# A tenth unit in the first phase, a third group buffer for one raw tile, later dt and gate transposes, first sums on VectorE

## The chip, the cores and the metric

The kernel runs on one core of a Trainium2 chip. The metric is the device time of one execution in microseconds (us). All tensors are float32 in HBM. Every weight is split on the core into a high and a low part, and each product is made of three matmuls.

## The reference, cut to what matters

Two layers work on 256 tokens of width 2048. Each layer scales and shifts its normalised input by values that come from a conditioning vector `c` through a large matrix `ada_w` (2048 by 6144), then runs a token mixer and a projection back.

```python
cond = silu(c)
for i in range(2):
    shift, scale, gate = split(cond @ ada_w[i] + ada_b[i], 3)
    h = rmsnorm(x, norm_w[i]) * (1 + scale) + shift
    out = ssd_mixer(h) if i == 0 else mlstm_mixer(h)
    x = x + gate * out
return rmsnorm(x, final_norm_w)

# ssd_mixer: proj = h @ w_in gives z, x, B, C (causal conv and silu on x, B, C) and dt
dt = softplus(dt + dt_bias); a = -exp(a_log) * dt      # per head; cumulated over tokens
y  = chunked scan over (x*dt, a, B, C) + d_skip * x    # 8 groups of 8 heads
out = rmsnorm_per_group(y * silu(z)) * norm_w @ w_out

# mlstm_mixer: proj = h @ w_in gives q, k, v, o, z and two gate rows per head
log_f = log_sigmoid(f_pre + b); decays from cumulated log_f and i_pre
out = (per-head norm of sigmoid(o) * chunked attention) * silu(z) @ w_out
```

## The kernel before

The weights arrive as loads of 512 KB, `raw` tiles of 128 by 1024 floats, on the queue of SyncE (SP). `RAWB` says how many raw tiles there are. A weight tile is split by ScalarE (`hi`, line 78, in `act`) and VectorE (`lo`, line 86, in `vtt`); there are four buffers of each. TensorE then runs 24 matmul triples of 256 columns for one half of an item (lines 304 to 306). An `ada` tile isn't split: VectorE multiplies it by a column of `cond` and adds it to the accumulator `aacc` (line 82, in `stt`).

Everything is one list of items, in `items`. A unit is four blocks of 128 output columns over the whole depth of 2048; it has four items of 1 MB (two loads each). In layer 0 the units are `z`, `x` (per group of eight heads) and `bc` (B and C of two groups).

- The first phase runs through the depth in four stages (`START`). A stage needs four chunks of the normalised input, `hT`, and these need eight `ada` items to be added up, transposed and summed (`total`, lines 233 to 257). Within a stage each unit of the list `PRE` gets one item, and the `ada` items of the next stage lie between them. The first two units of `PRE` stay in PSUM; of the others, each stage's part is added by VectorE to a `park` tile in SBUF. Those parked tiles are taken from the four `y` buffers, two units to a tile.
- The dt unit runs at the front of the last stage. `dt_done` makes softplus, decay and cumulated sums on VectorE, then transposes them on TensorE (lines 570 to 572).
- `POST` lists what follows: the other units and the output passes (`op`), with `ada` items (third entry of a token) spread among them. The scan of a group needs its `xs` tile, tag `s4b`, handed out in order of groups.
- Layer 1 begins in the same way, with the list `K1` and 16 late `ada` items among its items; `gates_done` is its counterpart to `dt_done`, with transposes on line 872.

Steps that belong to no matmul are generators. `run_bg` takes one step of each before every half item, so `yield from lag(n)` puts the next step n halves later in the program. The order on each engine is made from the program by a scheduler that can move a step ahead again; `tc.high_priority` puts what is written under it first. The engines then run their instructions in order.

Of the kernel before, what the change touches and what calls it, by code (L numbers as in the profile page):

```python
# [13 lines left out]
P = 128  # L14
T = 256
# [10 lines left out]
for _n, _w in _VEC:  # L26
# [6 lines left out]
START = [4, 4, 4, 4]  # L33
K1 = [("o", 0), ("z", 0), ("qk", 0), ("v", 0), ("qk", 1), ("v", 1), ("o", 1), ("z", 1)]
RES1, DEF1, GPOS = 2, 16, 0
PRE = [('x', 0), ('bc', 0), ('z', 0), ('x', 1), ('bc', 1), ('bc', 2), ('z', 1), ('x', 2), ('z', 2)]
RES = 2
RAWB, HIB, E6B = 6, 4, 2
HP_SPLIT = (False, None)
HP_OP = (True, None)  # L40
CONV_STT, NW_STT, Y_STT, OP_STT, X_DVE = True, False, False, True, False
ROWLAG = 4
LOOK_LOAD, LOOK_SPLIT, HALF_US, BG_LIM, BG_MIN, DEBT_CAP = 3, 3, 2.56, 3.0, 5, 2.0
HP_H = (True, None)
POST = [('z', 4), ('z', 3, (0, 1)), ('x', 3, (0, 1)), ('x', 4, (0, 2)), ('z', 5, (0, 2)), ('x', 5, (0, 2)),
        ('op', (0, 1, 2), (0, 8)), ('bc', 3), ('x', 6, (1, 1)), ('z', 6, (1, 1)), ('x', 7, (1, 1)), ('z', 7, (1, 1)),
        ('op', (3, 4), (1, 4)), ('op', (5, 6, 7), (1, 8))]

# [2 lines left out]
def trunk_kernel(ctx, tc, xt, vecs, ada, wdt, wss, wso, wgt, wml, wmo, fnw, result):  # L51
# [12 lines left out]
    def nm(s):  # L64
        uid[0] += 1
        return f"{s}{uid[0]}"
# [131 lines left out]
            gens.insert(0, b)  # L198
        return b

    slots = {"s4a": 2, "s4b": 2, "s4c": 2}

    def take(tag):
        yield from gate_ok(lambda: slots[tag] > 0)
# [9 lines left out]
    def ada_work(it):  # L214
        layer, key, q, w = it["layer"], it["key"], it["q"], it["w"]
        per = 1024 // w
        if q == 0:
            finish(sums)
            acc_tiles[layer, key] = sp.tile([P, 1024], F32, tag="adaacc", name=nm("aacc"), bufs=1)
        acc = acc_tiles[layer, key][:, 0:w]  # L220
        for k in range(2 * per * q, 2 * per * (q + 1)):
            raw = it["raw"][(k // per) % 2][:, (k % per) * w:(k % per + 1) * w]
            if k == 0:
                vts(acc, raw, cond[:, 0:1], None, ALU.mult)
            else:
                stt(acc, raw, cond[:, k:k + 1], acc, ALU.mult, ALU.add)
        if q != it["nq"] - 1:
            return
        if key < 4:
            spans = [(4 * key, 4), (16 + 4 * key, 4)]  # L230
        else:
            spans = [(32 + 8 * (key - 4), 4), (36 + 8 * (key - 4), 4)]
        def total():
            yield
            sm = sp.tile([P, 8], F32, tag="asum", name=nm("asum"))
            ps = [misc() for _ in spans]
            c = 0
            for t, (o, n) in zip(ps, spans):
                for b in range(n):
                    nc.tensor.transpose(t[:, b * P:(b + 1) * P], acc[:, (c + b) * P:(c + b + 1) * P], ident)  # L240
                c += n
            c = 0
            for t, (o, n) in zip(ps, spans):
                both = layer == 0 and key < 4 and c == 0
                if both:
                    nc.vector.tensor_reduce(sm[:, 0:n], t.rearrange("p (b t) -> p b t", b=4), axis=mybir.AxisListType.X,
                                            op=ALU.add)
                for b in range(0 if both else n):
                    sl = slice(b * P, (b + 1) * P)
                    act(t[:, sl], t[:, sl], AF.Copy, accum_out=sm[:, c + b:c + b + 1])  # L250
                m = mod[layer][:, o:o + n]
                vtt(m, sm[:, c:c + n], vec(f"ab{layer}", o, n), ALU.add)
                c += n
                known.update((layer, o + b) for b in range(n))
                if 16 <= o < 32:
                    stt(amul[layer][:, o - 16:o - 16 + n], m, 1.0, vec(f"nw{layer}", o - 16, n), ALU.add, ALU.mult)
            yield
        sums.append(spawn(total()))
# [288 lines left out]
    def dt_done(banks):  # L547
        def g():
            bk = banks[0][:, 0:T]
            rw = sp.tile([P, 4, T], F32, tag="a4", name="dtrow")  # L550
            dt, tmp = rw[:, 0, :], rw[:, 1, :]
            vts(tmp, bk, vec("dtb"), None, ALU.add)
            softplus(tmp, dt)
            yield
            na = sp.tile([P, 1], F32, tag="na", name="na", bufs=1)
            act(na, vec("alog"), AF.Exp)
            vts(na, na, -1.0, None, ALU.mult)
            vts(tmp, dt, na, None, ALU.mult)
            for c in range(2):
                s = slice(c * P, (c + 1) * P)  # L560
                nc.vector.tensor_tensor_scan(acs[:, s], ones, tmp[:, s], 0.0, ALU.mult, ALU.add)
            nc.gpsimd.dma_start(acd, acs[0:64, :])
            slots.update(a4=1, e6=2)
            spawn(gen_rows())
            cr = tmp[:, 0:P]
            vts(cr, acs[:, 0:P], -1.0, acs[:, P - 1:P], ALU.mult, ALU.add)
            yield
            p1, p2 = misc(), misc()
            for c in range(2):
                nc.tensor.transpose(p1[:, c * P:(c + 1) * P], dt[:, c * P:(c + 1) * P], ident)  # L570
                nc.tensor.transpose(p2[:, c * P:(c + 1) * P], acs[:, c * P:(c + 1) * P], ident)
            nc.tensor.transpose(p2[:, 2 * P:3 * P], cr, ident)
            give("a4")
            vts(dtT, p1[:, 0:T].rearrange("p (c h) -> p c h", c=2)[:, :, 0:64],
                                    0.5, None, ALU.mult)
            nc.vector.tensor_copy(acT, p2[:, 0:384].rearrange("p (c h) -> p c h", c=3)[:, :, 0:64])
            spawn(gen_decay())
            yield
        held["dt"] = spawn(g())
# [23 lines left out]
    def xs_done(g):  # L603
        def f(banks):
            def conv():
                yield from gate_ok(lambda: g == 0 or g - 1 in taken)
                yield from take("s4b")
                taken.add(g)
                xs_t[g] = sp.tile([P, 4, T], F32, tag="s4b", name=nm("xs"))
                yield from gen_conv(banks, "scw", "scb", [4 * g + b for b in range(4)], xs_t[g])  # L610
            x_done[g] = hold(spawn(conv()), banks)
            held[0, g] = spawn(gen_ssd(g))
        return f
# [233 lines left out]
    def gates_done(banks):  # L847
        def g():
            bk = banks[0][:, 0:T]
            rw = sp.tile([P, 4, T], F32, tag="a4", name="gaterow")  # L850
            xx, lf = rw[:, 0, :], rw[:, 1, :]
            ip = sp.tile([P, T], F32, tag="t1", name="ip", bufs=3)
            vts(xx, bk, vec("gb"), None, ALU.add)
            nc.vector.memset(ip, 0.0)
            act(ip[0:8, :], xx[32:40, :], AF.Copy)
            yield
            vts(xx, xx, -1.0, None, ALU.mult)
            softplus(xx, lf)
            yield
            vts(lf, lf, -1.0, None, ALU.mult)  # L860
            for_scan = sp.tile([P, T], F32, tag="t1", name="onesr", bufs=3)
            nc.vector.memset(for_scan, 1.0)
            bc = xx
            nc.vector.tensor_tensor_scan(bc, for_scan, lf, 0.0, ALU.mult, ALU.add)
            vtt(ip, ip, bc, ALU.subtract)
            nc.vector.tensor_tensor_scan(G, ip, ip, 0.0, ALU.max, ALU.max)
            nc.gpsimd.dma_start(Gd, G[0:8, :])
            vtt(lf, bc, G, ALU.add)
            yield from lag(6)
            p1, p2 = misc(), misc()  # L870
            for c in range(2):
                nc.tensor.transpose(p1[:, c * P:(c + 1) * P], lf[:, c * P:(c + 1) * P], ident)
                nc.tensor.transpose(p2[:, c * P:(c + 1) * P], ip[:, c * P:(c + 1) * P], ident)
            act(eT, p1[:, 0:T].rearrange("p (c h) -> p c h", c=2)[:, :, 0:8], AF.Exp, scale=-1.0)
            vts(ncT, p2[:, 0:T].rearrange("p (c h) -> p c h", c=2)[:, :, 0:8], -1.0, None, ALU.mult)
            yield
        held["gates"] = spawn(g())
# [27 lines left out]
    def o_done(h):  # L905
        def f(banks):
            head_over(h)
            to_t[h] = sp.tile([P, 4, T], F32, tag="s4b", name=nm("to"))
            for i in range(2):
                act(to_t[h][:, 2 * i:2 * i + 2, :], pair(banks[i]), AF.Tanh, scale=0.5)  # L910
        return f
# [94 lines left out]
    for q in range(4):  # L1006
# [4 lines left out]
        for j, w in enumerate(new):  # L1011
            if q == 3 and j == GPOS:
                add_unit(Unit("fm", 1, 8, 1, h_act, gates_done), [wgt])
            items.append(w)
            n = -(-len(late) // max(1, len(new) - j + (2 - q) * len(new))) if q < 3 and (q, j) >= (0, 3) else 0
            items.extend(late[:n])
            late = late[n:]
    assert not late
# [24 lines left out]
    def prep(j):  # L1043
        n, half = halves[j]
        it = items[n]
        if it["kind"] == "h":
            finish(sums)
            for k in it["ks"]:
                h_chunk(it["layer"], k)
            return  # L1050
        while nload[0] < min(len(loads), it["ln"] + LOOK_LOAD):
            load(loads[nload[0]])
# [114 lines left out]
```

## Time and profile before

| what | value |
|---|---|
| three runs | 1775.24 us median, 1775.02 to 1779.06 |
| profiled execution, its time | 1770.52 us |
| its span, first to last instruction | 1768.7 us |
| TensorE (PE) busy | 1679.2 us, 95% |
| VectorE (DVE) busy | 1301.9 us, 74% |
| ScalarE (ACT) busy | 923.3 us, 52% |
| read from HBM | 400.89 MB |
| mean granted clock of TensorE | 0.98 of full speed |

The profiled execution was 4.7 us faster than the median of the runs. TensorE is nearly always busy, so the time can only fall where TensorE waits, and it waits in the first half of the span for the most part. The two numbers to hold side by side in a stretch are the busy times of TensorE and VectorE.

### The profile page before, as it was taken

To read this page: it belongs to the slowest core of one execution; us is meant where nothing else is said; L and a number is where in the kernel's file an instruction comes from. 1 tells how busy PE (TensorE), PEld (TensorE's weight loads), DVE (VectorE), ACT (ScalarE), POOL (GpSimd) and SP (SyncE) were. 2 spreads that over 40 slices of the span, in tenths; PEclk is the share of its full clock that TensorE was granted. 3 is DMA by queue.
4 is the path that set the end of the run, shared out by engine and by line. 5 is a ranking of instruction groups with operands and counts; after the bars stand their busy time and mean duration, and the time that the engine had idled before them with its cause. 6 is when DMAs were issued, how large, how long until landed. Compare 5 with 4: busy or idle time off the path is not lost.

```text
span 1768.7 us, 32784 instructions
## 1 busy us (share of the span) xinstructions
PE 1679.2 (95%) x13285; PEld 1623.4 (92%) x13285; DVE 1301.9 (74%) x1639; ACT 923.3 (52%) x1551; POOL 35.6 (2%) x55
## 2 busy tenths in 40 slices
PE   2998979999999999989998999999999999999997
PEld 2998969998999999989888989899999898989997
DVE  7889978998986888867977986766556565564554
ACT  3443558788874674444445554544344444454433
POOL 0000000000000000000000000000000000000000
PEclk6999989999999999999999999999999999999998
DMA  9989745686876667958974567777555555565551
GB/s 358 338 311 320 275 161 179 213 280 226 280 284 207 220 219 254 337 167 307 328 249 153 203 229 246 254 246 246 182 181 178 181 175 184 188 196 169 189 180 71
DMA packets 111048, 405.20 MB, mean 229 GB/s; under 512 B 12440, under 2 KB 12448, under 8 KB 110896
## 3 DMA queue, kind: packets, MB, share of 16 engines
q1 hardware_dynamic: 107568, 391.50, 64.6%
q0 software_dynamic: 3040, 10.56, 2.0%
q8 instruction: 104, 1.70, 0.4%
q10 hardware_dynamic: 288, 1.05, 0.1%
q14 instruction: 48, 0.39, 0.1%
HBM read 400.89 MB, written 2.17 MB: 228 GB/s over the span
## 4 chain that ended last, share of the span: by engine, by line
PE 73%; issue 9%; DVE 8%; DMA 7%; ACT 2%; POOL 0%; SPq 0%; POOLq 0%; DVEq 0%; ACTq 0%
PE pj L304 18%; PE pj L305 18%; PE pj L306 18%; DMA raw<-in_ada 4%; DVE aacc L82 3%; DVE lo L86 3%; PE ms L304 2%; PE ms L305 2%; PE ms L306 2%; PE pj L315 2%; PE pj L317 2%; PE pj L316 2%; DMA raw<-in_wml 1%; ACT hi L78 1%; PE ms L697 1%
## 5 line engine op out<-in xcount | busy, mean ns | idle before, releaser
L78 ACT ACTIVATE hi<-raw 128x1024 fp32r<-128x1024 f32 x548 | 580.0, 1061 | 647.5 <-PE pj L305 394.0
L86 DVE TENSOR_TENSOR lo<-raw,hi 128x1024 fp32r<-128x1024 f32 x548 | 667.5, 1221 | 328.9 <-ACT hi L78 326.0
L304 PE MATMUL pj<-hT,hi 128*128 128x256 f32 x2144 | 605.3, 283 | 9.0 <-ACT hT L78 6.4
L305 PE MATMUL pj<-hT,hi 128*128 128x256 f32 x2144 | 600.3, 280 | 0.6 <-DVE hT L82 0.6
L306 PE MATMUL pj<-hT,lo 128*128 128x256 f32 x2144 | 600.0, 280 | 0.1
L304 PEld LDWEIGHTS pj<-hT,hi 128*128 128x128 f32 x2144 | 405.1, 189 | 12.2 <-ACT hT L78 7.2
L305 PEld LDWEIGHTS pj<-hT,hi 128*128 128x128 f32 x2144 | 405.1, 189 | 1.2 <-DVE hT L82 0.8
L306 PEld LDWEIGHTS pj<-hT,lo 128*128 128x128 f32 x2144 | 404.8, 189 | 0.3 <-DVE lo L86 0.3
L304 PE MATMUL pj<-y,hi 128*128 128x256 f32 x1024 | 291.4, 285 | 0.0
L306 PE MATMUL pj<-y,lo 128*128 128x256 f32 x1024 | 289.8, 283 | 0.0
L305 PE MATMUL pj<-y,hi 128*128 128x256 f32 x1024 | 289.8, 283 | 0.0
L82 DVE SCALAR_TENSOR_TENSOR aacc<-raw,cond,aacc 128x1024 f32<-128x1024 f32 x180 | 230.4, 1280 | 54.1 <-DMA raw<-in_ada 52.7
L304 PE MATMUL ms<-hT,hi 128*128 128x256 f32 x704 | 199.8, 284 | 9.4 <-ACT hi L78 3.3
L305 PE MATMUL ms<-hT,hi 128*128 128x256 f32 x704 | 197.6, 281 | 0.0
L306 PE MATMUL ms<-hT,lo 128*128 128x256 f32 x704 | 197.2, 281 | 0.0
L304 PEld LDWEIGHTS pj<-y,hi 128*128 128x128 f32 x1024 | 196.4, 192 | 0.5 <-issue 0.5
L305 PEld LDWEIGHTS pj<-y,hi 128*128 128x128 f32 x1024 | 196.5, 192 | 0.2 <-issue 0.2
L306 PEld LDWEIGHTS pj<-y,lo 128*128 128x128 f32 x1024 | 196.4, 192 | 0.0
L304 PEld LDWEIGHTS ms<-hT,hi 128*128 128x128 f32 x704 | 133.7, 190 | 12.1 <-ACT hi L78 4.6
L305 PEld LDWEIGHTS ms<-hT,hi 128*128 128x128 f32 x704 | 133.7, 190 | 0.3
L306 PEld LDWEIGHTS ms<-hT,lo 128*128 128x128 f32 x704 | 133.4, 190 | 0.0
L315 PE MATMUL pj<-hi,hT 128*128 128x512 f32 x192 | 76.5, 399 | 0.0
(186 smaller groups left out, 1549.3 us busy)
## 6 DMA issues: line engine op xcount, KB each, us to landing
raw<-in_wml SPq DMA_DIRECT2D x256, 512.0 KB, 4.2
raw<-in_ada SPq DMA_DIRECT2D x192, 512.0 KB, 5.3
raw<-in_wss SPq DMA_DIRECT2D x160, 512.0 KB, 4.8
raw<-in_wso SPq DMA_DIRECT2D x64, 512.0 KB, 5.8
raw<-in_wmo SPq DMA_DIRECT2D x64, 512.0 KB, 3.7
acb<-acd POOLq DMA_DIRECT2D x16, 512.0 KB, 5.6
xT<-in_xt SPq DMA_DIRECT2D x4, 512.0 KB, 5.9
raw<-in_wdt SPq DMA_DIRECT2D x2, 512.0 KB, 5.7
```

What stands on the lines that cost most here:

```text
L78: nc.scalar.activation(out, in_, func, **kw)
L82: nc.vector.scalar_tensor_tensor(out, a, s, b, op0, op1)
L86: nc.vector.tensor_tensor(out, a, b, op)
L304: nc.tensor.matmul(o, hi[:, w0:w0 + P], ah, start=first, stop=False, skip_group_check=True)
L305: nc.tensor.matmul(o, hi[:, w0:w0 + P], al, start=False, stop=False, skip_group_check=True)
L306: nc.tensor.matmul(o, lo[:, w0:w0 + P], ah, start=False, stop=last, skip_group_check=True)
L315: nc.tensor.matmul(o, ah[:, s], wh, start=(fresh and kk == 0), stop=False)
L316: nc.tensor.matmul(o, al[:, s], wh, start=False, stop=False)
L317: nc.tensor.matmul(o, ah[:, s], wl, start=False, stop=(kk == u.nk - 1 and (closes or (u.park is not None and ends))))
L697: nc.tensor.matmul(o, X[:, 0, xh, :], E[:, h, 0:T], start=True, stop=False, skip_group_check=True)
```

## The change

Eight edits. `('x', 3)` becomes the tenth unit of `PRE` and leaves `POST`; the `ada` item that was spread over it goes to `('x', 4)`. The raw tiles go from 6 to 5. The tag `s4b` gets a third buffer, in layer 0 (`xs`) and in layer 1 (`to`). The transposes of dt are put four yields instead of one after the sums, those of the gates eight instead of six. In the first phase both halves of the sums of an `ada` column block are made by one VectorE reduction each; before, the second half was four ScalarE copies with an accumulator. And in layer 0 the steps that finish sums and make `hT` are written under high priority. And in the count of late `ada` items for each item of `K1`, 2 is subtracted from a denominator.

```diff
-PRE = [('x', 0), ('bc', 0), ('z', 0), ('x', 1), ('bc', 1), ('bc', 2), ('z', 1), ('x', 2), ('z', 2)]
+PRE = [('x', 0), ('bc', 0), ('z', 0), ('x', 1), ('bc', 1), ('bc', 2), ('z', 1), ('x', 2), ('z', 2), ('x', 3)]
-RAWB, HIB, E6B = 6, 4, 2
+RAWB, HIB, E6B = 5, 4, 2
-POST = [('z', 4), ('z', 3, (0, 1)), ('x', 3, (0, 1)), ('x', 4, (0, 2)), ('z', 5, (0, 2)), ('x', 5, (0, 2)),
+POST = [('z', 4), ('z', 3, (0, 1)), ('x', 4, (0, 3)), ('z', 5, (0, 2)), ('x', 5, (0, 2)),
-    slots = {"s4a": 2, "s4b": 2, "s4c": 2}
+    slots = {"s4a": 2, "s4b": 3, "s4c": 2}
...
-                both = layer == 0 and key < 4 and c == 0
+                both = layer == 0 and key < 4
                 if both:
-                    nc.vector.tensor_reduce(sm[:, 0:n], t.rearrange("p (b t) -> p b t", b=4), axis=mybir.AxisListType.X,
+                    nc.vector.tensor_reduce(sm[:, c:c + n], t.rearrange("p (b t) -> p b t", b=4), axis=mybir.AxisListType.X,
                                             op=ALU.add)
...
             vts(cr, acs[:, 0:P], -1.0, acs[:, P - 1:P], ALU.mult, ALU.add)
-            yield
+            yield from lag(4)
             p1, p2 = misc(), misc()
...
-                xs_t[g] = sp.tile([P, 4, T], F32, tag="s4b", name=nm("xs"))
+                xs_t[g] = sp.tile([P, 4, T], F32, tag="s4b", name=nm("xs"), bufs=3)
...
             vtt(lf, bc, G, ALU.add)
-            yield from lag(6)
+            yield from lag(8)
...
-            n = -(-len(late) // max(1, len(new) - j + (2 - q) * len(new))) if q < 3 and (q, j) >= (0, 3) else 0
+            n = -(-len(late) // max(1, len(new) - j + (2 - q) * len(new) - 2)) if q < 3 and (q, j) >= (0, 3) else 0
...
-            finish(sums)
-            for k in it["ks"]:
-                h_chunk(it["layer"], k)
+            with prio(it["layer"] == 0):
+                finish(sums)
+                for k in it["ks"]:
+                    h_chunk(it["layer"], k)
```

**The dt transposes on TensorE.** `pj_2256` (after: `pj_2436`) is the bank of the dt unit. Before, the transposes stand right behind its last matmul:

```order
L304 MATMUL pj_2256<-hT,hi_2188 128x256
L305 MATMUL pj_2256<-hT,hi_2188 128x256
L306 MATMUL pj_2256<-hT,lo_2189 128x256
L570 MATMUL ms_2408<-ident,dtrow 128x128 x2
L571 MATMUL ms_2409<-ident,acs 128x128 x2
L572 MATMUL ms_2409<-ident,dtrow 128x128
L304 MATMUL ms_2493<-hT,hi_2363 128x256
```

Now one item (two halves, 48 matmuls into the banks `ms_2662` and `ms_2663`, unit `z` of group 0) stands between:

```order
L306 MATMUL pj_2436<-hT,lo_2369 128x256
L304 MATMUL ms_2662<-hT,hi_2543 128x256
...
L306 MATMUL ms_2663<-hT,lo_2580 128x256
L570 MATMUL ms_2704<-ident,dtrow 128x128 x2
L571 MATMUL ms_2705<-ident,acs 128x128 x2
L572 MATMUL ms_2705<-ident,dtrow 128x128
L304 MATMUL ms_2752<-hT,hi_2618 128x256
```

The transposes moved back by 48 matmuls, though the program put them three more halves (72 matmuls) later.

**The dt chain on VectorE.** `dtrow` and `spw` are the chain of dt, `bc` and `xs` convolutions, `lo` splits, `park` additions of the first phase. Before, from the chain's first row:

```order
L90 TENSOR_SCALAR dtrow<-pj_2256,V 128x256
L82 SCALAR_TENSOR_TENSOR bc_2485<-pj_361,V,bc_2485 128x254
L82 SCALAR_TENSOR_TENSOR spw_2319<-dtrow 128x256
L86 TENSOR_TENSOR lo_2482<-raw_2283,hi_2481 128x1024
L90 TENSOR_SCALAR spw_2319<-spw_2319 128x256
L82 SCALAR_TENSOR_TENSOR bc_2485<-pj_361,V,bc_2485 128x253
L419 RECIPROCAL spw_2319<-spw_2319 128x256
L82 SCALAR_TENSOR_TENSOR bc_2485<-th_2565,bc_2485 128x512
L86 TENSOR_TENSOR spw_2319<-spw_2319 128x256
L82 SCALAR_TENSOR_TENSOR xs_2403<-pj_300,V,xs_2403 128x254
```

Now, from the fourth row of the chain's stretch on:

```order
L86 TENSOR_TENSOR lo_2651<-raw_2463,hi_2650 128x1024
L90 TENSOR_SCALAR spw_2499<-spw_2499 128x256
L82 SCALAR_TENSOR_TENSOR bc_2654<-pj_358,V,bc_2654 128x253
L419 RECIPROCAL spw_2499<-spw_2499 128x256
L86 TENSOR_TENSOR lo_2693<-raw_2539,hi_2692 128x1024
L86 TENSOR_TENSOR spw_2499<-spw_2499 128x256
L86 TENSOR_TENSOR park_496<-park_496,ms_2662 128x512
L86 TENSOR_TENSOR spw_2499<-spw_2499 128x256
L86 TENSOR_TENSOR park_496<-park_496,ms_2663 128x512
L90 TENSOR_SCALAR spw_2499<-spw_2499 128x256
L86 TENSOR_TENSOR lo_2742<-raw_2541,hi_2741 128x1024
```

From the chain's first row to its last there are now three splits instead of one and two `park` additions instead of none; one convolution row has left. The rows of the convolutions and of the chain are the same otherwise.

**The gate transposes on TensorE.** `ms_11083` and `ms_11084` are the banks of a unit of layer 1 that stands before them in both. Before:

```order
L317 MATMUL ms_11084<-lo_11005,hT 128x512
L872 MATMUL ms_11130<-ident,gaterow 128x128
L873 MATMUL ms_11131<-ident,ip 128x128
L872 MATMUL ms_11130<-ident,gaterow 128x128
L873 MATMUL ms_11131<-ident,ip 128x128
L304 MATMUL ms_11141<-hT,hi_11041 128x256
```

Now the next item (48 matmuls, the same that stood behind them) comes first:

```order
L305 MATMUL ms_11136<-hT,hi_11076 128x256
L306 MATMUL ms_11136<-hT,lo_11077 128x256
L872 MATMUL ms_11203<-ident,gaterow 128x128
L873 MATMUL ms_11204<-ident,ip 128x128
L872 MATMUL ms_11203<-ident,gaterow 128x128
L873 MATMUL ms_11204<-ident,ip 128x128
L315 MATMUL ms_11215<-hi_11103,hT 128x512
```

On VectorE the chain of the gates has the same rows between its first and its last as before. On the SP queue the order of the loads of layer 1 is the same in both programs, row for row.

## Rows read from the trace of the kernel before

**Rows 1.** The page: busy time, share of the span and instructions of each engine.
```profile
PE 1679.2 (95%) x13285; PEld 1623.4 (92%) x13285; DVE 1301.9 (74%) x1639; ACT 923.3 (52%) x1551; POOL 35.6 (2%) x55
```

**Rows 2.** Who TensorE waited for, longest first: us in total, times, longest.
```profile
PE ms L240 <- DVE aacc L82: 22.5, 6, 15.3
PE ms L570 <- DVE dtrow L82: 12.9, 1, 12.9
...
PE ms L872 <- DVE gaterow L86: 5.3, 1, 5.3
PE ms L304 <- ACT hi L78: 3.3, 1, 3.3
...
PE pj L304 <- DVE xs L82: 2.6, 1, 2.6
```

**Rows 3.** Windows: us from the span's start, length, busy us by engine, clock, DMA share, GB/s.
```profile
95.00:152.00 57.00, 53.59 (x452) 52.80 (x452) 51.19 (x57) 22.89 (x31) 0.00 (x0) 1.00 0.93 330
152.00:209.00 57.00, 53.55 (x441) 52.91 (x440) 51.52 (x60) 23.68 (x32) 0.00 (x0) 0.97 0.88 308
...
243.00:300.00 57.00, 55.75 (x479) 54.20 (x479) 44.86 (x58) 47.63 (x114) 2.73 (x5) 1.00 0.59 192
300.00:436.00 136.00, 132.63 (x1138) 129.53 (x1137) 126.92 (x168) 112.03 (x248) 9.50 (x11) 1.00 0.71 239
...
780.00:900.00 120.00, 111.99 (x828) 105.70 (x829) 99.80 (x115) 55.74 (x96) 0.00 (x0) 0.97 0.85 299
...
1000.00:1768.70 768.70, 755.80 (x5791) 726.25 (x5789) 470.40 (x583) 353.18 (x466) 11.02 (x16) 0.99 0.58 194
```

**Rows 4.** TensorE in order of time around the dt transposes: start, length, instruction, idle before.
```profile
225.38 0.28 PE L306 MATMUL pj<-hT,lo 128*128 128x256 f32 x1
...
226.43 0.27 PE L306 MATMUL pj<-hT,lo 128*128 128x256 f32 x1
239.59 0.69 PE L570 MATMUL ms<-ident,dtrow 128*128 128x128 f32 x2 [12.89 <-DVE dtrow L82]
...
241.67 0.41 PE L306 MATMUL ms<-hT,lo 128*128 128x256 f32 x1
...
243.16 0.36 PE L304 MATMUL ms<-hT,hi 128*128 128x256 f32 x1
```

**Rows 5.** VectorE in order of time: a first sum, then the dt chain.
```profile
34.62 0.69 DVE L246 TENSOR_REDUCE asum<-ms 128x4 f32<-128x512 f32 x1 [1.27 <-PE ms L240]
...
226.74 0.48 DVE L90 TENSOR_SCALAR dtrow<-pj,V 128x256 f32<-128x256 f32 x1 [0.20 <-PE pj L306]
...
227.87 1.22 DVE L86 TENSOR_TENSOR lo<-raw,hi 128x1024 fp32r<-128x1024 f32 x1
...
240.62 0.26 DVE L90 TENSOR_SCALAR dtrow<-acs 128x128 f32<-128x128 f32 x1
...
247.31 1.36 DVE L86 TENSOR_TENSOR park<-park,ms 128x512 f32<-128x512 f32 x2
```

**Rows 6.** TensorE in order of time behind the gate transposes.
```profile
962.68 0.44 PE L872 MATMUL ms<-ident,gaterow 128*128 128x128 f32 x1 [5.33 <-DVE gaterow L86]
...
966.76 0.37 PE L304 MATMUL ms<-hT,hi 128*128 128x256 f32 x1
```

**Rows 7.** Loads issued on line 264 from 780 to 900 us, and who waited for them.
```profile
L264 SPq DMA_DIRECT2D raw<-in_wml x37: 327/328/328, 789.6 to 895.8; - x37
L264 SPq DMA_DIRECT2D raw<-in_ada x30: 327/328/328, 791.6 to 885.3; - x30
...
  ACT hi L78: 30.5, 14
  DVE aacc L82: 12.3, 8
...
DMA to landing us min/median/max: 3.1/5.8/7.9
```

More of the change, by code (lines that the diff above doesn't have):

```diff
@@ L907, in f @@
             head_over(h)
-            to_t[h] = sp.tile([P, 4, T], F32, tag="s4b", name=nm("to"))
+            to_t[h] = sp.tile([P, 4, T], F32, tag="s4b", name=nm("to"), bufs=3)
             for i in range(2):
```

## The prediction

> **What bounds the kernel now.** I read the busy times first: TensorE is busy for 95% of the span, VectorE for 74% [rows 1]. Behind 1000 us TensorE is at work for 755.8 of 768.7 us, so nothing there can fall by much; what can fall lies ahead of it [rows 3]. The second view is who TensorE waited for [rows 2]. Of the 22.5 us for `aacc`, 15.3 is one wait at the start, for the first eight `ada` items, which no edit here shortens. Then come one wait of 12.9 us for the dt row and one of 5.3 us for the gate row. The third view is the windows. In the second and third stage of the first phase (57 us each) TensorE is busy 53.6 us and VectorE 51.2 and 51.5 us [rows 3]: two engines close to each other. From 300 to 436 us VectorE is busy for 126.9 of 136 us. So in the first 436 us a wait that is taken from TensorE is worth only as much as VectorE can follow.
>
> The order of time shows what a wait costs besides its length [rows 4]. Nine matmuls ahead of the dt wait take from 225.38 to 226.43, 0.117 us each. Behind it, seven take from 241.67 to 243.16, 0.213 us each: from its restart at 239.59 until 243.16 TensorE is at the lower of its two clock levels (1.2 instead of 2.4 GHz), and of these 3.6 us some 45% are lost, about 1.5 us. At the gates the last long matmul begins 4.1 us behind the restart [rows 6].
>
> **The change part by part.** All durations are of the profiled execution, 1770.5 us.
>
> *Tenth unit.* A stage gets one more item: 48 matmuls of 0.117 us, 5.6 us on TensorE. VectorE gets two splits of 1.22, two `park` additions of 1.36 together and the second sum of 0.69 [rows 5]: 4.5 us, so some 55.7 us for a stage. Now a stage lasts 57.0 us while nine items need 50.5 and the transposes 0.9: TensorE loses 5.6 us, of which the longest piece is 3.3 us for a split that came late [rows 2]. If the 5.8 us that VectorE idles in a stage stay, the stage will take 61.5 us, against 57.0 that TensorE needs, and the loss is 4.5 us: 1.1 gained. If VectorE's idle time goes, the whole 5.6 us is gained. The two stages between them give 2 to 11 us; I take 4, near the lower end, since VectorE and TensorE need nearly the same and neither ever ran without idle time in these rows.
>
> *dt transposes.* On VectorE the chain lasts from 226.74 to 240.88, 14.1 us [rows 5]. The new order puts two more splits (2.4 us) and one pair of `park` additions (1.4 us) among its rows and takes a 0.5 us step out: 17.4 us. On TensorE only 48 matmuls stand between, 5.6 us, not the three halves more that the program asks for. So the wait from dt's last matmul to the last transpose falls from 14.1 to 11.8 us: 2.3 gained. Should VectorE be through sooner because the mixed-in work is done earlier, it is 5.6. It is all 12.9 us plus 1.5 of clock only if the chain takes less than half of what it does. I take 2.5. Behind the transposes wait the scan's factors, `acT` and `dtT`, for which group 0 waits; it will start about 17 us later in TensorE's work than now.
>
> *Units after dt.* x3's four items (22.5 us) leave this stretch, and the scan's work on VectorE stays. From 243 to 436 us VectorE idles 21 us in 193 [rows 3]. The shorter stretch takes nearly all of that. Against it, the third group buffer lets a convolution leave PSUM earlier; the wait for `xs` is 2.6 us [rows 2]. I take 0, with 5 lost or 5 gained as the ends.
>
> *Gate transposes.* The chain's rows on VectorE are the same as now; on TensorE one item, 5.6 us, now fills the 5.33 us wait [rows 6]. Its splits stand ahead of the chain's last rows, so they are ready. With the clock that is 5.3 + 1.5 = 6.8 us gained. At worst the wait keeps half of its length and the clock falls all the same: 3 gained.
>
> *Five raw tiles.* No row shows five. The dense stretch from 780 to 900 us makes 67 loads in 106 us, one in 1.58 us; six tiles then turn over in 9.5 us, of which 5.8 is from issue to landing (3.1 at least) and 3.7 is from landing until the split or the addition is over [rows 7]. ScalarE and VectorE wait 30.5 and 12.3 us for loads there, so a slower load is felt; and on SP's queue a load that waits for a free tile holds all loads behind it, weights and `ada` alike. With five tiles and the same turnover the pace is one in 1.90 us: 21 us lost. If the landing shortens by what one load fewer in the queue takes, half of 5.8 - 3.1 = 1.35 us, the turnover is 8.15 us, the pace 1.63, and 3.4 us are lost. If it shortens in full proportion, nothing is. I take 3.5 here and, as the stages of the first phase load at 308 to 330 GB/s [rows 3] but wait for VectorE more than for loads, 1.5 there: 5 lost, ends 0 and 21.
>
> *No cost.* The first sum on VectorE (0.69 us) delays the first `hT` by as much as putting three `hT` steps ahead of a 1.22 us split saves [rows 5]. The denominator changes no row: the order of loads of layer 1 is the same. `to`'s third buffer lies where TensorE is full.
>
> The sum: 0 - 4 - 2.5 + 0 - 6.8 + 5 = -8.3 us, so 1762.2. The runs' median lies 4.7 above the profiled execution; on that scale it is 1767.
>
> **The rivals.** *Raw tiles decide (slower).* Loads fall behind in the first phase and from 780 to 900 us, some 220 us, in which ScalarE already waits for them [rows 7]. The gains sum to 13.3 us; they are used up when the pace falls by 6%, and it is slower by 0.3% (5.3 us, about what a measurement of this kernel can tell from no change) from 8.5% on. At 10%: 22 - 13 = 9 us, 1784. For it speaks that five tiles are a sixth fewer; against it, 2.7 us of queue in the landing that can shrink.
>
> *VectorE gives the pace.* What the stages and dt gain is lost again between 243 and 436 us, where VectorE is at 93%; the gates' 6.8 and the tiles' 5 cancel: 1773.
>
> *The waits go wholly.* VectorE follows; dt gives 14.4, the stages 11, the units after dt 5, the gates 6.8, the tiles cost 5: -32, 1743. Against it, the place of the dt transposes.
>
> *Loads at the memory's own pace.* If the stretches at 308 to 330 GB/s are held by the memory and not by tiles, a tile fewer costs nothing: -13.3, 1762. Speaks for it: a DMA share of 0.88 to 0.93 [rows 3]; against: the pace follows the releases. The Trainium skill, "DMA: Bandwidth & Descriptors", Specifications, gives a core's share of HBM as about 358 GB/s; by that the stages are at 86 to 92% of the limit and a lost tile would matter little. The trace agrees in part: a load lands after 5.8 us in the dense stretch and after 3.1 at best [rows 7].
>
> **How the numbers follow.** Chances: the forecast 0.36 (1761 to 1772); memory's pace 0.10; waits go wholly 0.14; VectorE's pace 0.20; raw tiles 0.20. Faster by over 0.3% (below 1769.9): 0.30 of the forecast's, all of the second and third: 0.54. Slower (above 1780.6): 0.15 of the tiles' case, and 0.02 of VectorE's, if the units after dt lose more than the 5 us. Within: the rest, 0.29. The range from 1750 to 1783 leaves out half of the third case and a third of the last.
>
> **What would show it.** Right: the gate wait is under 1 us and no matmul at 0.213 us follows; the dt wait is 6 to 9 us by itself; the second and third stage take 60 to 62 us with VectorE busy some 55.5; the waits of ScalarE for `wml` from 780 to 900 us grow past 30.5 us and the waits for `aacc` there by 3 us. Wrong: a dt wait near zero, stages of 57 us, or a stretch from 780 to 900 us that is longer by 8 us or not at all.

## The result, and the profile after

| | median us | runs | profiled execution, its time | its span |
|---|---|---|---|---|
| before, on the same chip | 1775.13 | 1773.84 to 1779.06 | 1770.52 | 1768.7 |
| after | 1796.01 | 1790.68 to 1798.85 | 1798.85 | 1797.1 |

The ratio is 1.011, with a 95% interval of 1.0079 to 1.0142: some 20 us slower, where the forecast was 8 us faster and the range ended at 1783. Below, a ratio is always against runs of the kernel before on the same chip (its medians there lay between 1775 and 1779 us), and "us" is that ratio times 1775.

The page of the changed kernel, busy time of each engine (beside [rows 1]). TensorE is busy for 12.7 us longer with the same 13285 matmuls: its mean granted clock is 0.974 instead of 0.980 of full speed, and 0.6% of 1690 us is 10 us.

```profile
PE 1691.9 (94%) x13285; PEld 1633.3 (91%) x13285; DVE 1311.5 (73%) x1649; ACT 917.9 (51%) x1521; POOL 34.1 (2%) x55
```

Who TensorE waited for (us in total, times, longest; beside [rows 2]). The dt wait is 9.3 instead of 12.9 us, the gate wait has no row any more, and the wait of 2.6 us for `xs` at line 304 has gone too (two others for `xs`, of 1.5 and 1.2 us, are there). Longer or new are the waits for `aacc` and `hi`, both made from loads, and for `park`, the addition that frees a bank of PSUM.

```profile
PE ms L240 <- DVE aacc L82: 26.3, 5, 16.2
...
PE ms L570 <- DVE dtrow L82: 9.3, 1, 9.3
PE ms L304 <- DVE park L86: 7.4, 5, 3.4
...
PE ms L304 <- ACT hi L78: 4.3, 3, 3.1
PE pj L304 <- ACT hi L78: 3.9, 2, 3.5
PE ms L304 <- ACT park L78: 3.0, 2, 2.2
...
```

Windows of the changed kernel (length, busy us of PE, PEld, DVE, ACT, POOL, clock, DMA share, GB/s; beside [rows 3]). In the same stretches of the first phase the rate of the loads fell from 330 and 308 to 279 and 276 GB/s, and VectorE and TensorE both do less. The second and third stage, from one set of `ada` transposes to the next, are 71.5 and 66.5 us long; VectorE is busy for 56.7 and 56.3 us of them. The forecast had 61.5 each, with VectorE at 55.5: its work was about right, the length was not. (By the same marks the kernel before has 60.4 and 56.6 us; the 57 us of the prediction were windows, not stages.)

```profile
90.70:162.20 71.50, 65.19 (x538) 64.36 (x536) 56.70 (x63) 29.59 (x35) 0.00 (x0) 0.98 0.83 285
162.20:228.70 66.50, 61.04 (x488) 59.03 (x488) 56.34 (x64) 22.28 (x24) 0.00 (x0) 0.97 0.83 285
...
95.00:152.00 57.00, 52.39 (x431) 51.78 (x431) 44.40 (x49) 23.38 (x29) 0.00 (x0) 0.97 0.81 279
152.00:209.00 57.00, 50.02 (x398) 48.21 (x397) 48.04 (x57) 17.57 (x19) 0.00 (x0) 0.97 0.82 276
...
300.00:436.00 136.00, 133.68 (x1151) 130.43 (x1150) 131.73 (x185) 115.52 (x258) 6.73 (x9) 1.00 0.67 228
```

TensorE in order of time around the dt transposes (beside [rows 4]), then behind the gate transposes (beside [rows 6]). At dt TensorE waits 9.29 us and then 0.71 more; behind it TensorE is again at the lower of its clock levels, 0.21 us from matmul to matmul until 281.95 and 0.12 from there, where it is at 2.4 GHz. At the gates there is no wait, and the matmuls behind a pause of 1.13 us for `eT` follow each other after 0.23 to 0.24 us with 512 columns each, the higher level from the second on.

```profile
266.03 0.28 PE L306 MATMUL ms<-hT,lo 128*128 128x256 f32 x1
275.60 0.66 PE L570 MATMUL ms<-ident,dtrow 128*128 128x128 f32 x2 [9.29 <-DVE dtrow L82]
276.97 0.70 PE L571 MATMUL ms<-ident,acs 128*128 128x128 f32 x2 [0.71 <-DVE acs L561]
...
281.73 0.38 PE L305 MATMUL ms<-hT,hi 128*128 128x256 f32 x1
281.95 0.29 PE L306 MATMUL ms<-hT,lo 128*128 128x256 f32 x1
282.08 0.28 PE L304 MATMUL ms<-hT,hi 128*128 128x256 f32 x1
```

```profile
992.73 0.28 PE L306 MATMUL ms<-hT,lo 128*128 128x256 f32 x1
992.85 0.27 PE L872 MATMUL ms<-ident,gaterow 128*128 128x128 f32 x1
...
994.93 0.50 PE L315 MATMUL ms<-hi,hT 128*128 128x512 f32 x1 [1.13 <-ACT eT L78]
995.27 0.40 PE L316 MATMUL ms<-hi,hT 128*128 128x512 f32 x1
995.51 0.40 PE L317 MATMUL ms<-lo,hT 128*128 128x512 f32 x1
```

On VectorE the chain of dt [rows 5] now runs from 260.75 to 277.32, 16.6 us; 17.4 was worked out. Its first and last row:

```profile
260.75 0.48 DVE L90 TENSOR_SCALAR dtrow<-pj,V 128x256 f32<-128x256 f32 x1 [0.21 <-PE pj L306]
...
277.06 0.26 DVE L90 TENSOR_SCALAR dtrow<-acs 128x128 f32<-128x128 f32 x1
```

The loads at the start of layer 1 (beside [rows 7]; the same 67 loads, counted along the queue, now begin 27 us later, so the window does too, from 816 to 932 us). From the first issue to the last they take 115.1 us instead of 106.2, 8.9 us more; the landing fell by 0.3 us, and the waits for the loads did not grow. The prediction had named longer waits as its sign, and a stretch longer by 8 us as the sign against it.

```profile
L264 SPq DMA_DIRECT2D raw<-in_wml x37: 327/328/328, 816.5 to 931.6; - x37
L264 SPq DMA_DIRECT2D raw<-in_ada x30: 327/328/328, 818.3 to 914.7; - x30
...
  ACT hi L78: 29.9, 11
  DVE aacc L82: 12.1, 7
...
DMA to landing us min/median/max: 3.2/5.5/8.0
```

### The profile page after: what moved, and what is told of

It reads as the page before. It is cut to its first block, busy times and chain, and to the rows that moved or that the text cites. A ratio compares the mean times of both kernels' runs of the same rounds, so it can differ in the third digit from the quotient of the medians.

```text
span 1797.1 us, 32766 instructions
## 1 busy us (share of the span) xinstructions
PE 1691.9 (94%) x13285; PEld 1633.3 (91%) x13285; DVE 1311.5 (73%) x1649; ACT 917.9 (51%) x1521; POOL 34.1 (2%) x55
## 4 chain that ended last, share of the span: by engine, by line
PE 66%; DMA 11%; DVE 11%; issue 10%; ACT 2%; POOL 0%; SPq 0%; POOLq 0%; DVEq 0%; ACTq 0%
PE pj L304 15%; PE pj L306 15%; PE pj L305 15%; DMA raw<-in_ada 6%; DVE aacc L82 4%; DVE lo L86 4%; PE ms L304 3%; PE ms L306 3%; PE ms L305 3%; DMA raw<-in_wso 2%; PE pj L315 2%; PE pj L316 2%; PE pj L317 2%; DMA raw<-in_wss 2%; ACT hi L78 1%
## 5 line engine op out<-in xcount | busy, mean ns | idle before, releaser
L304 PE MATMUL pj<-hT,hi 128*128 128x256 f32 x2080 | 587.3, 283 | 7.4 <-ACT hT L78 7.0
L306 PE MATMUL pj<-hT,lo 128*128 128x256 f32 x2080 | 582.3, 280 | 1.4 <-DVE lo L86 1.4
L305 PE MATMUL pj<-hT,hi 128*128 128x256 f32 x2080 | 582.1, 280 | 0.0
L304 PEld LDWEIGHTS pj<-hT,hi 128*128 128x128 f32 x2080 | 392.8, 189 | 10.2 <-ACT hT L78 7.7
L306 PEld LDWEIGHTS pj<-hT,lo 128*128 128x128 f32 x2080 | 392.4, 189 | 1.8 <-DVE lo L86 1.8
L305 PEld LDWEIGHTS pj<-hT,hi 128*128 128x128 f32 x2080 | 392.9, 189 | 0.4
L304 PE MATMUL ms<-hT,hi 128*128 128x256 f32 x768 | 220.6, 288 | 16.3 <-DVE park L86 7.4
L306 PE MATMUL ms<-hT,lo 128*128 128x256 f32 x768 | 218.3, 285 | 1.4 <-DVE lo L86 1.3
L305 PE MATMUL ms<-hT,hi 128*128 128x256 f32 x768 | 218.5, 285 | 0.0
L304 PEld LDWEIGHTS ms<-hT,hi 128*128 128x128 f32 x768 | 148.8, 194 | 20.0 <-DVE park L86 8.1
L306 PEld LDWEIGHTS ms<-hT,lo 128*128 128x128 f32 x768 | 148.9, 194 | 2.3 <-DVE lo L86 2.3
L305 PEld LDWEIGHTS ms<-hT,hi 128*128 128x128 f32 x768 | 149.1, 194 | 0.4
```

The lines of the kernel that those rows point to most:

```text
L304: nc.tensor.matmul(o, hi[:, w0:w0 + P], ah, start=first, stop=False, skip_group_check=True)
L305: nc.tensor.matmul(o, hi[:, w0:w0 + P], al, start=False, stop=False, skip_group_check=True)
L306: nc.tensor.matmul(o, lo[:, w0:w0 + P], ah, start=False, stop=last, skip_group_check=True)
```

## The experiments

Theory A: the raw tile cost far more than the 5 us given to it, by holding back the loads of the first phase; the other edits gain. Rivals: B, the tenth unit overloads VectorE and ScalarE, whatever the tiles; C, both together; later ones for single terms.

**e1: the change with six raw tiles, and two group buffers to make room.**

```diff
-RAWB, HIB, E6B = 5, 4, 2
+RAWB, HIB, E6B = 6, 4, 2
-    slots = {"s4a": 2, "s4b": 3, "s4c": 2}
+    slots = {"s4a": 2, "s4b": 2, "s4c": 2}
```

(and `bufs=3` of `xs` and `to` taken out)

> The changed kernel with six raw tiles again, and for the room the third group buffer taken back to two; all other edits stay. Theory A (five raw tiles starve the loads; the other edits gain): 1760 to 1772 us, ScalarE's waits for wss loads in the second and third stage fall from some 40 us to 20, the stages take 62 us instead of 71 and 66. Theory B (the tenth unit gives VectorE and ScalarE too much in the first phase, whatever the tiles): 1785 to 1797 us with the stages still at 66 us or more. Theory C (both together): in between, near 1780.

1782.48 us, ratio 1.0023 (1.0008 to 1.0038). The raw tile gives most of the loss back, but the result is not faster than before: that is what C expected (near 1780), and A's 1760 to 1772 was missed. The waits of TensorE from 400 to 460 us show why: two of a length that neither the kernel before (2.6 and 0.6 us for `xs`) nor the changed one (1.5) has.

```profile
PE ms L348 <- DVE xs L86: 6.0, 1, 6.0
PE pj L304 <- ACT ms L78: 5.2, 1, 5.2
```

**e2: the kernel before with five raw tiles alone** (`RAWB` 6 to 5).

> The kernel before with five raw tiles and nothing else changed. Theory A: 1790 to 1800 us, the stages of the first phase 60 us or more instead of 57, and 8 us or more lost from 690 to 900 us. Theory B: 1774 to 1780 us, stages as before. Theory C: 1780 to 1788 us.

1799.95 us, ratio 1.0117 (1.0097 to 1.0138): 21 us. This one number makes as much as the whole change. For the raw tile theory A holds; by B alone the time would have stayed.

**e3: the change with nine units in the first phase** (`PRE` and `POST` of before).

> The changed kernel with the two lists of units of the kernel before, so nine units in the first phase; five raw tiles and three group buffers stay. Theory A: still 1785 to 1800 us, with the loss of the layer 1 stretch unchanged. Theory B: 1765 to 1777 us. Theory C: 1777 to 1787 us.

1796.12 us, ratio 1.0104 (1.0085 to 1.0123). With five raw tiles, nine or ten units make no difference.

**e4: the kernel before with the tenth unit alone** (`PRE` and `POST` of the change).

> The kernel before with the two lists of units of the changed kernel, so a tenth unit in the first phase; six raw tiles, nothing else changed. Theory A: 1765 to 1775 us, stages of 61 to 63 us. Theory B: 1785 to 1797 us, stages of 66 us or more. Theory C: 1777 to 1785 us.

1790.21 us, ratio 1.007 (1.0052 to 1.0088): 12 us lost with six raw tiles. Theory A expected a gain; the time lies in B's range. The stages last 67.9 and 61.8 us, but the largest piece is the pair of waits of e1, 6.0 and 5.2 us between 400 and 460 us: with x3 done early, the scan's groups come closer together, and two group buffers are not enough (e12 has three and lacks these waits).

**e5: the kernel before with the gate transposes later, alone.**

```diff
             vtt(lf, bc, G, ALU.add)
-            yield from lag(6)
+            yield from lag(8)
```

> The kernel before with the gate transposes eight yields instead of six after the scan, nothing else changed. Theory D (the wait of 5.3 us and the slower clock behind it are gained, as in the sum of the prediction): 6 to 7 us faster, about 1769 us. Theory E (what needs the transposed gates comes later by the same item and waits in turn, at the exponentials right behind and at the first matmuls of the chunked attention): within 2 us of the kernel before.

1770.39 us, ratio 0.9959 (0.9942 to 0.9975): 7.3 us, the 6.8 of the sum. A little comes back as new waits of 1.1 us (`eT`) and 1.0 us (`dg`), not enough for theory E.

**e6: the kernel before with the dt transposes later, alone** (`yield` becomes `yield from lag(4)`).

> The kernel before with the dt transposes four yields instead of one after the sums, nothing else changed. Theory D: the wait falls from 12.9 us to 6 to 9.5 us and 2.5 to 6 us are gained, 1769 to 1773 us. Theory E (group 0 starts later by the item that was put ahead, and VectorE, nearly full up to 436 us, gives the end of this stretch): within 2 us of the kernel before.

1773.06 us, ratio 0.9965 (0.995 to 0.9979): 6.2 us, at least 3.7. The wait falls from 12.9 to 9.2 us, and one of 0.7 us for `acs` (0.2 before) stands behind it: 3.2 of the 6.2 us are explained. The wait for `xs` falls from 2.6 to 1.9.

**e7: the change with six raw tiles and three group buffers, the room taken from the `lo` tiles** (three instead of four).

> The changed kernel with six raw tiles and three group buffers; the room comes from the lo tiles, three instead of four. Theory F (the tenth unit needs the third group buffer, the raw tile was the price): 1762 to 1772 us, no wait of more than 2 us for xs near 420 us. Theory G (three lo tiles hold ScalarE and VectorE back as much as five raw tiles do): 1785 us or more.

1791.05 us, ratio 1.0055 (1.0034 to 1.0076): theory G, for the most part. Against e12 below, which differs by the `lo` tile and helper tiles, the fourth `lo` tile is worth 1.1%, 20 us: a raw tile is free only when its `lo` is made, and from 50 to 200 us the rate of the loads is 296 GB/s, little more than with five raw tiles (286 in the changed kernel). So e7 alone says nothing on the group buffer.

**e8: the kernel before with seven raw tiles and three `lo` tiles.**

> The kernel before with seven raw tiles, the room taken from the lo tiles, three instead of four. Theory A (the pace of the loads goes with the number of tiles at six too): 5 to 12 us faster, the loads of the second and third stage at 340 GB/s or more. Rival (at six tiles the memory or the split gives the pace): within 3 us of the kernel before or slower, stages still at 57 us.

1781.3 us, ratio 1.0016 (1.0005 to 1.0028). Inconclusive for the time, as the missing `lo` tile costs: neither the 5 to 12 us nor the 340 GB/s of theory A came. The rate from 50 to 200 us is 328 GB/s, against 320 in the kernel before and 318 in e13, a small step up. That the memory can give more, a row further below shows.

**e9: the change with two group buffers and five raw tiles.**

> The changed kernel with two group buffers instead of three; five raw tiles, the tenth unit and all else stay. Theory F (with ten units the scan's groups come closer together and the third group buffer is worth 10 to 14 us between the dt transposes and 460 us): 1802 to 1812 us, with waits of 4 to 6 us for xs near 440 us. Theory H (the loads give the pace with five tiles, and a late xs costs nothing more): 1794 to 1799 us.

1803.03 us, ratio 1.0125 (1.0103 to 1.0147), against 1.011 of the change: 2.7 us more, within the intervals. The waits of theory F are there (7.0 and 4.0 us for `xs` at 437 and 446 us), yet little of them is left at the end, which is nearer to theory H (the median itself, 1803, is at the foot of F's range; as a ratio it makes 1797). How the rest is caught up wasn't tested. Against e1, the raw tile is worth 1.0%, 18 us, with two group buffers.

**e10: the kernel before with all first sums on VectorE and the sums and `hT` steps under high priority.**

> The kernel before with both halves of the first sums on VectorE and the sums and hT steps under high priority, nothing else changed. The prediction's step (no cost, no gain): within 2 us of the kernel before, the first hT as late. Rival: the reordering in the first phase gains or loses by the order of splits, 4 us or more either way.

1780.93 us, ratio 1.0002 (0.9988 to 1.0015). No cost, no gain, as in the sum.

**e11: the kernel before with both later transposes, gates and dt, and nothing else.**

> The kernel before with the two later transposes of the change, gates and dt, and nothing else. If the two gains of the single runs (7.3 and 6.2 us by their ratios) add: 1761 to 1768 us, ratio 0.991 to 0.994. If the dt gain is only the spread of runs: ratio 0.995 to 0.997.

1765.02 us, ratio 0.9919 (0.9894 to 0.9944): 14 us faster, and the two gains add. This version beats both kernels. Who TensorE waits for in it: what is left of dt, and no gates.

```profile
PE ms L240 <- DVE aacc L82: 22.9, 6, 15.3
...
PE ms L570 <- DVE dtrow L82: 9.3, 1, 9.3
...
PE ms L304 <- ACT hi L78: 3.5, 1, 3.5
...
```

**e12: the whole change with six raw tiles.** Room comes from small helper tiles (and some tiny ones).

```diff
-RAWB, HIB, E6B = 5, 4, 2
+RAWB, HIB, E6B = 6, 4, 2
...
-                    m = sp.tile([P, 384], F32, tag="cbm", name=nm("cbm"), bufs=3)
+                    m = sp.tile([P, 384], F32, tag="cbm", name=nm("cbm"), bufs=2)
...
-        dg = sp.tile([P, T], F32, tag="gb", name=nm("dg"), bufs=3)
+        dg = sp.tile([P, T], F32, tag="gb", name=nm("dg"), bufs=2)
...
-        tmp = sp.tile([P, T], F32, tag="t1", name=nm("htmp"), bufs=3)
+        tmp = sp.tile([P, T], F32, tag="t1", name=nm("htmp"), bufs=2)
```

> The changed kernel with six raw tiles and three group buffers; the room comes from helper tiles (the tags cbm, gb and t1 have two buffers instead of three). Theory A (all that the change lost is the raw tile): 1758 to 1768 us, ratio 0.990 to 0.996, no wait of over 3 us for xs near 420 us. Theory I (the tenth unit gains nothing, since VectorE gives the pace of the stages and of the stretch behind dt): ratio 0.997 to 1.003.

**e13: the kernel before with the same helper tiles.**

> The kernel before with the same smaller helper tags (cbm, gb and t1 with two buffers instead of three), as a measure of what this costs. If they don't matter: ratio 0.998 to 1.002. If they hold the chunked scan or the norms back: 1.003 to 1.010, with new waits behind 250 us.

e13: 1776.02 us, ratio 1.0 (0.9983 to 1.0018); the helper tiles cost nothing that can be measured. e12: 1766.09 us, ratio 0.9943 (0.9928 to 0.9957), 10 us faster. The loads stand in the same order on SP's queue as in the changed kernel, row for row (on TensorE, VectorE and ScalarE the number of tiles also moves some rows, as it does between e2 and the kernel before). So the change with its raw tile back is faster than before, and the tile with the order that it brings turns -10 us into +20: 30 us (1.011 - 0.9943 = 0.0167; about 6 us either way by the intervals). That is more than the 21 us of e2 and the 18 of e9 against e1: the price of the tile depends on what else the kernel has. Against e1 the third group buffer is worth 0.8%, 14 us, and the two waits near 425 us are gone. TensorE's waits of e12 from 260 to 500 us:

```profile
PE ms L570 <- DVE dtrow L82: 9.3, 1, 9.3
PE pj L304 <- ACT hi L78: 2.0, 1, 2.0
PE ms L571 <- DVE acs L561: 0.7, 1, 0.7
PE ms L348 <- DVE xs L86: 0.6, 1, 0.6
...
```

**e14: the kernel before with four raw tiles** (`RAWB` 6 to 4).

> The kernel before with four raw tiles. Theory A, by turnover: from six to five the rate of the loads in the first phase fell from 318 to 331 GB/s to 284 to 301, some 10%, and 21 us were lost. With four tiles in the air and a load of 5.5 us from issue to landing the rate falls by 15 to 20% more, and TensorE has no slack left to hide it: 55 to 100 us lost, ratio 1.03 to 1.06. Rival (what six to five lost is a change of order, not of rate): ratio below 1.02.

1870.21 us, ratio 1.0528 (1.0511 to 1.0544): 94 us. The second tile costs three and a half times as much as the first. The same window of the first phase, 50 to 200 us, with six tiles (the kernel before), five (e2) and four (e14), and under each the time from issue to landing:

```profile
50.00:200.00 150.00, 142.22 (x1195) 141.06 (x1194) 132.25 (x142) 65.43 (x88) 0.00 (x0) 0.99 0.91 320
...
DMA to landing us min/median/max: 4.1/5.6/7.1
```

```profile
50.00:200.00 150.00, 136.21 (x1086) 133.28 (x1085) 119.75 (x128) 58.87 (x82) 0.00 (x0) 0.95 0.86 292
...
DMA to landing us min/median/max: 3.1/5.5/7.2
```

```profile
50.00:200.00 150.00, 130.44 (x981) 127.42 (x981) 109.18 (x115) 55.07 (x78) 0.00 (x0) 0.91 0.80 267
...
DMA to landing us min/median/max: 3.2/5.2/7.2
```

Read three columns together. The rate is 320, 292 and 267 GB/s. The matmuls in the window are 1195, 1086 and 981: they fall by 9.1 and 9.7%, the rate by 8.8 and 8.6%. So in this phase the progress of the kernel is the progress of the loads. TensorE's busy time hides that: it falls by 4% a step only, as its clock sinks from 0.99 to 0.91 and each matmul takes longer. The landing stays where it was, 5.6, 5.5 and 5.2 us.

**e15: both transposes later, dt at eight yields instead of four.**

> The kernel before with the gate transposes at eight yields and the dt transposes at eight instead of four; on TensorE 141 matmuls then stand ahead of the dt transposes, 16.5 us, more than the chain of 14 to 17 us lasts. If the wait is what counts: no dt wait, 4 to 9 us faster than the kernel with four yields, ratio 0.987 to 0.990. If group 0 and VectorE give the end of this stretch: ratio 0.991 to 0.995, with new waits for xs near 425 us.

1767.69 us, ratio 0.9951 (0.9935 to 0.9968); e11 has 0.9919 (0.9894 to 0.9944). The dt wait is wholly gone and nothing more is gained by it. Between 240 and 460 us TensorE waits elsewhere, 7.0 us in three places:

```profile
PE ms L304 <- DVE dtT L90: 3.0, 1, 3.0
PE ms L304 <- DVE cbm L82: 2.1, 1, 2.1
PE pj L304 <- DVE xs L82: 1.9, 1, 1.9
...
```

## Why the prediction was wrong

**Where the time went.** Between marks on TensorE (the first projection matmul, the dt transposes, the first line 315 of layer 1, the gate transposes, the end) the profiled executions took, in us:

| stretch | before | after | e12: after, six tiles | e2: before, five tiles |
|---|---|---|---|---|
| to the first projection | 40.8 | 42.6 | 41.7 | 43.1 |
| first phase, to dt | 198.8 | 233.0 | 218.0 | 214.0 |
| dt to layer 1 | 561.4 | 549.4 | 539.0 | 567.7 |
| layer 1 to the gates | 161.7 | 167.9 | 164.6 | 169.7 |
| gates to the end | 806.0 | 804.3 | 803.7 | 804.9 |

After and e12 differ by the raw tile and by helper tiles that cost nothing (e13). The tile's 30.0 us are 0.9, 15.0, 10.4, 3.2 and 0.5 in these stretches. These are single profiled executions, and that of the kernel before is a fast one (1770.5 us, where its medians are 1775 to 1779), so other pairs that differ by the raw tile are set beside it. The first phase gives the same in all: 15.2 us (e2 against before), 15.1 (e2 against e13), 14.7 (e9 against e1). The stretch from dt to layer 1 gives 6.3, 2.3 and 4.0 us there instead of 10.4, and layer 1 to the gates 8.0, 5.3 and 5.2 instead of 3.2. So the 15 us are firm, and how the rest divides is not.

**The step that failed: "Five raw tiles".** I took 5 us, 1.5 of them in the first phase and 3.5 from 780 to 900 us. The second part was of the right order at best: 3.2 to 8.0 us on TensorE by these pairs, though the loads of that stretch took 8.9 us longer and the waits for them did not grow. The first part was wrong by a factor of ten, 15 us, and a third part was missing: 2 to 10 us between dt and layer 1, where I had no term. In the changed kernel 7.9 of its 10.4 us lie between the `ada` transposes at 457 and at 767 us (309.9 us, against 302.0 in e12). The reason that I gave for the small value, that the stages "wait for VectorE more than for loads", was read from the busy times and from TensorE's waits. A view that points at the tiles is that of the DMA queue's own waits. For the kernel before, from 50 to 200 us (us in total, times, longest), its two largest rows are:

```profile
SPq L264 <- DVE lo L86: 59.9, 45, 3.9
SPq L264 <- DVE aacc L82: 43.8, 42, 3.5
```

For 103.7 of 150 us the queue held a load back until VectorE had freed a raw tile. This row alone doesn't tell whether tiles or VectorE give the pace: it is 102.3 us with five tiles (e2) and 95.9 with four (e14). What tells is the taking away of a tile. If VectorE were the bound, it would have been as busy as before; but its busy time in this window falls from 132.3 to 119.8 and 109.2 us, and the waits for the loads grow. Those of ScalarE for `wss`, before and after:

```profile
ACT hi L78 <- DMA raw<-in_wss: 24.8, 14, 6.4
```

```profile
ACT hi L78 <- DMA raw<-in_wss: 46.1, 17, 10.3
```

The model under the term was sounder than its use. Turnover is tiles in the air by 0.524 MB by the rate: 6 by 0.524 MB at 320 GB/s is 9.8 us, 5 at 292 is 9.0, 4 at 267 is 7.9. The first step shortened it by 0.9 us, not by the 1.35 that I took (with 1.35 the rate falls by 3%, with 0.9 by 9%); and it shortened in the time that a landed tile waits to be used, not in the landing (5.6, 5.5, 5.2 us). Of the rivals, "raw tiles decide" had the mechanism and the rate (a fall near 9%, where I had put its turning point at 8.5%), and 1784 instead of 1796: it counted 220 us of dense loads, so 22 us for the tile where e12 gives 30, and 13 us for the gains, of which e12 shows 10.

**The rival that fell: loads at the memory's own pace.** The rate follows the number of tiles, 267, 292 and 320 GB/s (e14, e2, before). And the kernel before itself loads faster where an `ada` tile is freed by one VectorE instruction and few weights are loaded: from 5 to 35 us its six tiles bring 408 GB/s, so the memory can give more than 320.

```profile
5.00:35.00 30.00, 8.39 (x41) 7.87 (x42) 20.94 (x21) 7.44 (x18) 1.67 (x1) 0.66 1.02 408
```

The Trainium skill gives 358 GB/s per core as the share when both cores of a pair stream, and says in "HBM Reference", Specifications (TRN2), that a core alone gets about 425. This kernel runs on one core; by that sentence the stages were at some 75% of the limit, an estimate, not at 86 to 92% as the prediction had it, and the 408 GB/s agree with it.

**Tenth unit.** I took -4, for the second and third stage. By the `ada` transposes these two stages are, in the kernel before and then in e12:

```profile
83.90:144.30 60.40, 57.69 (x488) 57.08 (x489) 53.49 (x60) 27.10 (x38) 0.00 (x0) 1.00 0.90 318
144.30:200.90 56.60, 52.51 (x430) 51.92 (x430) 51.49 (x60) 22.14 (x30) 0.00 (x0) 0.97 0.89 315
```

```profile
85.00:153.70 68.70, 63.87 (x537) 63.14 (x537) 56.95 (x63) 29.45 (x34) 0.00 (x0) 0.99 0.87 302
153.70:214.30 60.60, 59.14 (x488) 58.49 (x489) 55.47 (x65) 21.89 (x23) 0.00 (x0) 0.98 0.87 305
```

Together they last 117.0 and 129.3 us: 12.3 us more for 106 matmuls more, which are 12.4 us at 0.117 each. So nothing is gained in this pair. All kernels with nine units, six raw tiles and four `lo` tiles have 116 to 120 us here, those with ten 127 to 130 (e1, e4, e12), on average 10.7 us more, so perhaps 2 us of the 4 are there. The rest of the path agrees. Up to dt, e12 is 19.2 us longer with 192 matmuls (22.5 us) more, three items of x3 and the item of z that now stands ahead of the dt transposes (an item is 48 matmuls, 24 for a half, not 24 triples); of the 3.3 us between, the shorter dt wait makes 3.2. From dt to layer 1, 192 matmuls fewer save 22.4 us, as they should. What e12 has and e11 lacks (the tenth unit, the third group buffer, the sums) makes -14 into -10 us; the intervals overlap, so it is no gain that can be seen, and perhaps a loss of 4 us. And "units after dt: 0", right with the third group buffer, hid a condition: without the buffer that term is +14 us with six raw tiles (e1), far outside the 5 that I allowed, and 2.7 with five (e9).

**dt transposes.** From the last matmul ahead of them to the last transpose, 14.6 us became 11.4, where 11.8 was worked out (the waits within are 9.3 and 0.7 us); the chain took 16.6 us instead of 17.4. That is 3.2 us, but the gain was 6.2 us (3.7 to 8.9) instead of 2.5: right in kind, too small, and where the rest comes from no row shows. e15 shows the other end: with the wait gone wholly, nothing more comes, so "all 12.9" was not to be had by moving the transposes.

**Gate transposes** (-6.8; -7.3 measured, e5) and **no cost** for sums and priority (0; e10) were right.

The sum with measured terms: -7 for the gates, -6 for dt, 0 for the sums, +4 for the tenth unit with its buffer, +30 for the raw tile: +21, against +20 of the ratio. This is no independent check, as the last two terms are differences with e12 that must lead back to the changed kernel. By e2 alone the tile would be 21 us.

## What to carry to other kernels

Before a load buffer is given away, read the waits of the DMA queue itself: where the queue waits for free tiles most of the time, the rate of the loads is tiles by turnover, and the tiles may give the pace, whoever seems to free them. Taking one tile away tells: here the stretch then slowed in step with the rate, and the engine that frees the tiles became less busy. Compare the counts of matmuls in a window, not TensorE's busy time, which grows when the clock falls. Room for another buffer is best taken from helper tiles whose third copy nobody waits for (e13), and a wait that is moved entirely out of the way need not be worth its length (e11 against e15).

## What was not expected of the hardware

The landing of a 512 KB load hardly depends on how many can be in the air at once, four to six: 5.2, 5.5 and 5.6 us in the median, while the shortest, in the same window, is 3.2, 3.1 and 4.1. I had allowed 1.35 us less for one tile fewer. The two lower of the shortest fit what the Trainium skill says in "SBUF — State Buffer", The DMA setup-cost knee: about 2 us and the bytes at 436 GB/s, an estimate of 3.2 us for 512 KB. What makes the median so much longer with only four tiles was not tested.

The granted clock of TensorE sank with starved loads from 0.99 to 0.95 and 0.91 in that window (e2, e14), although no single wait of TensorE there was longer than 2.8 and 4.2 us; all its waits there come to 13.5 and 19.5 of 150 us (7.8 before).
